# Compression products in column quarters and attention scores in row halves, in one hybrid decoder layer

## The chip, the cores and the metric

The kernel is one program on one core of a Trainium2 chip. The metric is device time in microseconds of one execution; lower is better. Five engines work side by side and in order, each on its own list of instructions: TensorE (PE in the profile, its weight loads PEld), VectorE (DVE), ScalarE (ACT), GpSimd (POOL) and SyncE (SP), which here issues nearly all loads from DRAM. TensorE is an array of 128 rows (the summed dimension) by 128 columns (the columns of the held operand, which become the partitions of the result). A product that holds only 32 columns can be put in one quarter of the array's columns, and one that sums over only 64 partitions in one half of its rows.

## The reference, cut to what matters

The layer takes 256 tokens of 1024 features: an adaptive norm, one input projection, a retention group of 4 heads, an attention group of 8 query heads in 2 groups of keys and values (NSA) with compressed, selected and windowed branches, one output projection, a second adaptive norm, and a retrieval over 16384 experts (PEER). The change touches two places of the attention group:

```
def _compress(kraw, pe, w1, b1, w2):
    ...
    blk = kraw[:, idx] + pe[None, None, :, None, :]
    blk = blk.transpose(0, 1, 3, 2, 4).reshape(B, ncb, G, CMP_LEN * DH)
    return jax.nn.gelu(blk @ w1 + b1) @ w2
...
s_s = jnp.einsum('bqghd,bgqnkd->bghqnk', qblk, ksel).astype(f32) * scale
...
s_w = jnp.einsum('bqghd,bkgd->bghqk', qblk, kwb).astype(f32) * scale
```

There are 15 overlapping blocks of 32 tokens in each of the 2 groups, so `blk @ w1` has 30 rows; it sums over 2048 features into 256, once for keys and once for values. A head has 64 features. With 256 tokens every block of the selected branch that a query may see is selected, so both branches become causal attention over all keys.

## The kernel before, in words

The program is in two parts. The prefix (about the first 184 us) makes the norm, the projections, retention, attention, the output projection and the second norm. PEER follows and streams 16 weights `wq`, then 128 `down` and 128 `up` weights through TensorE. All of it stands in one function, `build`; nearly every instruction is recorded by line 80, so the profile's groups are told apart by the names of tiles.

Most of the prefix's matrix products are made from two parts: a float32 weight `raw` is split on ScalarE into a rounded `H` and on VectorE into the rest `L`, and three products (`H` by `hH`, `L` by `hH`, `H` by `hL`) go to a bank of PSUM, tag `C`. These splits can be done ahead, and their products are what TensorE does while a chain elsewhere is under way. The compression, the attention and the transposes use plain float32 products; the trace has two records for each of those and one for each transpose.

`compress` (lines 537 to 595) runs for keys, then for values. Eight small products per half turn the projected rows into columns; VectorE adds the position table and makes `blk` (128 partitions by 16 by 30). Then 16 products, with 30 columns of `blk` held and 256 columns of a quarter of `w_cmp` (tile `praw`) streamed, sum into one bank of tag `O`. ScalarE copies the 30 x 256 result to `hn`, two transposes turn it, and a chain of small steps on VectorE and ScalarE (`cu`, `cw`, tanh, `hid`) makes the gelu. Two more sets of small products give the compressed keys `kcT`, or the compressed values `vc`, which are spread into `vblk`.

`attn_unit(tt, p)` (line 635) makes the scores of heads p and 4 + p for the 128 queries of half tt, for both branches. `keys` holds the keys of group 0 in partitions 0 to 63 and of group 1 in 64 to 127, each with zeros in the other 64 partitions. In the first half (tt = 0) one product of 512 columns gives all four blocks of scores in one bank of tag `S`; a second, small one with `identb` and `negm` adds the causal mask. In the second half there is one product of 512 columns for each group, in a bank of its own. VectorE takes the maxima (`a_mx`), ScalarE the exponentials (`a_pr`, one of each branch and group, with their sums), VectorE the scales `a_sm`, ScalarE applies them, TensorE transposes, ScalarE copies (`a_pT`), and `attn_pv` sums over the values into a bank of tag `O` with products that hold 64 columns: group 0 goes to partitions 0 to 63, group 1 to 64 to 127, in turn. There are two banks each of the tags `S`, `T`, `C` and `O`.

Each engine's order is fixed when the program is built: a scheduler takes what it holds to be ready by its own costs, except in stretches where the code asks for program order. Between the attention it places the products `C` of the retention's values and gate, the splits, and on VectorE the sums of the adaptive norm's weights (`adaraw`), 128 x 1024 each, whose results are needed only at the end of the prefix.

Of the kernel before, what the change touches and what calls it, by code (L numbers as in the profile page):

```python
# [36 lines left out]
P = 128  # L37
# [11 lines left out]
PRAW = 3  # L49
# [14 lines left out]
def build(tc, I, out, dbg=None, stop=None):  # L64
# [5 lines left out]
    class Ordered:  # L70
        """An engine whose instructions stay in program order while order["on"] has its name."""
# [74 lines left out]
    def mm(o, a, b, start, stop):  # L146
        PE.matmul(o, a, b, start=start, stop=stop)
# [6 lines left out]
    def rstd_of(pool, ss, n, inv, tag):  # L154
        """1/sqrt(ss * inv + eps), a square root and one Newton step."""
# [13 lines left out]
    def rstd_pair(pool, sa, sb, tag, between=lambda: None):  # L169
        """Two factors of 1/sqrt((sa + sb) / D + eps): a square root's inverse and one Newton step."""  # L170
# [15 lines left out]
    # ------------------------------------------------------------------ prefix  # L186
# [11 lines left out]
    def table(func, dep=None):  # L198
        """Has a function's table loaded before a chain needs it, once dep is there."""
        t = mk(pers, (P, 1), F32, "tinyo", bufs=2)  # L200
        S.activation(t, tiny if dep is None else dep, func, scale=0.0)
# [29 lines left out]
    # 2 silu(c) on every partition  # L231
# [36 lines left out]
    # norm 1: the product that transposes a row block scales it too  # L268
# [38 lines left out]
    # projection blocks A (q | kc ks kw vc) and B (rq | vs vw gate)  # L307
# [92 lines left out]
    def rope(dst, src, tab, tt, nh, dh, v=0):  # L400
        """dst (SBUF) = rotated src (PSUM), nh heads of dh."""
# [24 lines left out]
    def half(c, post, nf=0):  # L426
        """A projection block of 512 columns; post(i) after each of its four units."""
# [56 lines left out]

    rr = {}
# [23 lines left out]
    # NSA transposes  # L509
    qT = mk(pe_, (P, 4, T), F32, "qT")  # L510
    keys = mk(pe_, (P, 2, 2, T), F32, "keys")
    G.memset(keys[64:, 0], 0.0)
    G.memset(keys[:64, 1], 0.0)
    for tt in range(2):
# [3 lines left out]
        for g in range(2):  # L518
            rows = slice(g * 64, (g + 1) * 64)
            S.activation(keys[rows, g, :, tt * P:(tt + 1) * P], b[rows, :256].rearrange("p (a b) -> p a b", a=2),  # L520
                         AF.Copy)
# [10 lines left out]
    # compressed keys and values  # L532
# [4 lines left out]
    def compress(kv):  # L537
        pe_t, b1_t, w2_t = cmpc[kv]
# [7 lines left out]
        blk = mk(wk, (P, 16, 2, 15), F32, "blk", bufs=1)  # L546
        for s in range(2):
            rows = slice(s * 64, (s + 1) * 64)
            bv = b[rows, :].rearrange("p (g t) -> p g t", g=2)
            for g in range(2):  # L550
                src = bv[:, g, s:s + 1]
                src = bass.AP(tensor=src.tensor, offset=src.offset, ap=[list(src.ap[0]), [2, 16], [16, 15]])
                V.tensor_tensor(blk[rows, :, g, :], src, pe_t[rows, :, None].to_broadcast([64, 16, 15]), op=ALU.add)
        b = bank("O")
        for i in range(4):
            key = ("w" + kv, i)
            load(key, I["w" + kv + "1"][:, i * 4:i * 4 + 4, :], (P, 4, 256))
            r, _ = raws.pop(key)
            for q in range(4):
                mm(b[:30, :256], blk[:, i * 4 + q].rearrange("p a b -> p (a b)"), r[:, q * 256:(q + 1) * 256],  # L560
                   i == 0 and q == 0, i == 3 and q == 3)
        hn = mk(wk, (32, 256), F32, "hn", bufs=1)
        S.activation(hn[:30, :], b[:30, :256], AF.Copy)
        b = bank("O")
        for ch in range(2):
            PE.transpose(b[:, ch * 32:ch * 32 + 30], hn[:30, ch * P:(ch + 1) * P], ident[:30, :30])
# [30 lines left out]
    compress("k")  # L597
    compress("v")
# [8 lines left out]
    # NSA attention  # L607
# [27 lines left out]
    def attn_unit(tt, p):  # L635
        """The scaled probabilities of heads p and 4 + p, transposed."""
# [6 lines left out]
        bs = []  # L643
        if tt == 0:
            b = bank("S")
            mm(b.rearrange("p (a b) -> p a b", a=4), qT[:, p, tq], keys.rearrange("p a b c -> p (a b) c")[:, :, :P],
               True, False)
            mm(b, identb, negm.rearrange("p a b -> p (a b)"), False, True)
            V.tensor_reduce(mx, b.rearrange("p (a b) -> p a b", a=4), axis=AX.X, op=ALU.max, negate=True)
            bs = [b, b]  # L650
        else:
            for g in heads:
                b = bank("S")
                o = b.rearrange("p (a b) -> p a b", a=2)
                mm(b, qT[:, p, tq], keys[:, g].rearrange("p a b -> p (a b)"), True, False)
                mm(o[:, :, P:], identb, negm[:, :2, :], False, True)
                V.tensor_reduce(mx[:, g * 2:(g + 1) * 2], o, axis=AX.X, op=ALU.max, negate=True)
                bs.append(b)
        w = P * (tt + 1)
        for g in heads:  # L660
            pr = mk(wk, (P, 2, T), F32, "a_pr", bufs=7)
            for br in range(2):
                src = bs[g][:, g * 256 + br * P:g * 256 + br * P + P] if tt == 0 else bs[g][:, br * T:(br + 1) * T]
# [47 lines left out]
    # retention: scores transposed, decayed  # L711
# [14 lines left out]
    # retention: values, group norm, swish gate  # L726
# [43 lines left out]
    # output projection, residual, norm 2: one half of the tokens after the other  # L770
# [79 lines left out]
    # ------------------------------------------------------------------- PEER  # L850
# [61 lines left out]
    def top_gen(sc):  # L912
        """Top 16 of each product key half, then of each head's candidates; then the tables."""
# [7 lines left out]
        for tt in range(2):  # L921
# [30 lines left out]
            # softmax over the 16, its maximum first in the sorted values  # L952
# [368 lines left out]
```

## Time and profile before

| | us |
|---|---|
| median of 3 runs (1039.6 to 1041.15) | 1039.87 |
| span of the profiled execution | 1037.9 |
| TensorE busy | 1009.2 |
| VectorE busy | 760.4 |
| ScalarE busy | 606.8 |
| GpSimd busy | 61.5 |

The profiled execution's own time was not kept apart from the runs; its span lies 2.0 us under their median. A page reads from the top: which engine is busy for which share, then the span in slices, then the chain that ended last. An engine that is busy for 97% can still be paced by another in a stretch, so the stretches are read one by one.

### The profile page before, as it was taken

The numbers are of one execution on the slowest core, as the hardware profiler recorded it, in microseconds if no ns is written. First come the engines' busy times: TensorE is split into PE (matmuls) and PEld (weight loads), VectorE is DVE, ScalarE is ACT, GpSimd is POOL, SyncE is SP. The second block draws the span as 40 slices with busy tenths as digits, with TensorE's granted clock in tenths as the row PEclk, the third lists the DMA queues.
The fourth block names the chain that finished last, engine by engine and source line by source line (L and its number), as shares of the span: only waits on it lengthen the run. The fifth ranks groups of instructions, "written<-read, shape, count | busy, mean of one in ns | idle before, by whom it ended". The sixth has DMA issues, their size and how long they took to land.

```text
span 1037.9 us, 17713 instructions
## 1 busy us (share of the span) xinstructions
PE 1009.2 (97%) x6580; PEld 902.1 (87%) x6582; DVE 760.4 (73%) x1653; ACT 606.8 (58%) x1244; POOL 61.5 (6%) x53
## 2 busy tenths in 40 slices
PE   7999999999998889999999999999999999999995
PEld 6876687999998889999999999988888888888884
DVE  7988888899778786667777777665955556565665
ACT  7544884555436357777777777645445555545453
POOL 1040000000331310000000000000000000000001
PEclk9999999999999999999999999999999999999998
DMA  9998753546555444444444444567976666666661
GB/s 367 352 350 335 244 181 136 168 152 183 168 149 174 144 152 135 151 147 143 148 142 144 143 143 143 156 230 231 317 234 193 197 190 214 190 199 188 198 189 57
DMA packets 56184, 199.19 MB, mean 192 GB/s; under 512 B 7305, under 2 KB 7585, under 8 KB 55713
## 3 DMA queue, kind: packets, MB, share of 16 engines
q1 hardware_dynamic: 55200, 193.59, 58.3%
q0 software_dynamic: 752, 4.20, 1.1%
q8 instruction: 51, 0.84, 0.3%
q14 instruction: 37, 0.30, 0.1%
q10 hardware_dynamic: 144, 0.26, 0.1%
HBM read 195.92 MB, written 2.11 MB: 191 GB/s over the span
## 4 chain that ended last, share of the span: by engine, by line
PE 84%; DVE 9%; POOL 3%; ACT 1%; issue 1%; DMA 0%; SPq 0%; DVEq 0%; POOLq 0%; ACTq 0%
PE acc L80 54%; PE dn L80 9%; PE w L80 7%; PE C L80 5%; PE O L80 4%; POOL oe L946 3%; PE S L80 3%; PE T L80 2%; DVE ev L80 2%; DVE L L80 2%; DVE oh L80 1%; DVE tp L80 1%; DVE VL L80 1%; DVE adaraw L80 0%; DMA xn<-in_x_dram 0%
## 5 line engine op out<-in xcount | busy, mean ns | idle before, releaser
L80 DVE TENSOR_TENSOR L<-raw,H 128x1024 fp32r<-128x1024 f32 x284 | 346.4, 1221 | 119.5 <-ACT H L80 114.9
L80 ACT ACTIVATE H<-raw 128x1024 fp32r<-128x1024 f32 x284 | 300.0, 1058 | 172.4 <-PE acc L80 132.6
L80 PE MATMUL acc<-H,a 128*128 128x512 f32 (+1 forms) x1030 | 315.9, 388 | 0.0
L80 PE MATMUL acc<-hH,H 128*128 128x256 f32 x800 | 230.8, 289 | 0.0
L80 PE MATMUL acc<-hH,L 128*128 128x256 f32 x800 | 226.6, 283 | 3.3 <-DVE L L80 3.3
L80 PEld LDWEIGHTS acc<-H,a 128*128 128x128 f32 x1030 | 193.0, 188 | 39.9
L80 PE MATMUL acc<-hL,H 128*128 128x256 f32 x800 | 226.6, 283 | 0.0
L80 PE MATMUL acc<-L,a 128*128 128x512 f32 (+1 forms) x515 | 199.7, 388 | 0.0
L80 PEld LDWEIGHTS acc<-hH,L 128*128 128x128 f32 x800 | 152.9, 191 | 4.1 <-DVE L L80 4.1
L80 PEld LDWEIGHTS acc<-hH,H 128*128 128x128 f32 x800 | 153.5, 192 | 0.1
L80 PEld LDWEIGHTS acc<-hL,H 128*128 128x128 f32 x800 | 153.2, 192 | 0.2 <-DVE hL L80 0.2
L80 PEld LDWEIGHTS acc<-L,a 128*128 128x128 f32 x515 | 96.7, 188 | 19.7
L80 ACT ACTIVATE ow<-o,VL 128x128 f16<-128x128 f16 x256 | 104.5, 578 | 5.2 <-DVE o L80 5.2
L80 PE MATMUL dn<-hH,L 128*128 128x256 f32 x352 | 99.8, 283 | 4.4 <-DVE L L80 4.4
L80 PE MATMUL dn<-hH,H 128*128 128x256 f32 x352 | 101.5, 288 | 0.4 <-ACT H L80 0.4
L80 PE MATMUL dn<-hL,H 128*128 128x256 f32 x352 | 99.6, 283 | 0.0
L80 PEld LDWEIGHTS dn<-hH,L 128*128 128x128 f32 x352 | 67.3, 191 | 5.0 <-DVE L L80 5.0
L80 PE MATMUL w<-ow,o 128*128 128x128 f16 x512 | 71.0, 296 | 0.0
L80 PEld LDWEIGHTS dn<-hH,H 128*128 128x128 f32 x352 | 67.6, 192 | 0.6 <-ACT H L80 0.6
L80 PEld LDWEIGHTS dn<-hL,H 128*128 128x128 f32 x352 | 67.4, 192 | 0.0
L80 PEld LDWEIGHTS <-o 128*128 128x128 f16 x512 | 51.9, 118 | 3.4
L80 DVE TENSOR_TENSOR ow<-o,VL 128x512 f16<-128x512 f16 x64 | 26.9, 420 | 36.9 <-PE w L80 36.9
(333 smaller groups left out, 1213.5 us busy)
## 6 DMA issues: line engine op xcount, KB each, us to landing
raw<-in_down_dram SPq DMA_DIRECT2D x128, 512.0 KB, 3.6
raw<-in_up_dram SPq DMA_DIRECT2D x128, 512.0 KB, 3.7
adaraw<-in_wadaT_dram SPq DMA_DIRECT2D x40, 512.0 KB, 8.0
raw<-in_wq_dram SPq DMA_DIRECT2D x16, 512.0 KB, 3.7
raw<-in_win_C_dram SPq DMA_DIRECT2D x12, 512.0 KB, 5.2
rawA<-in_win_A_dram SPq DMA_DIRECT2D x8, 512.0 KB, 9.6
raw<-in_wout_dram SPq DMA_DIRECT2D x8, 512.0 KB, 4.7
VL<-in_wadaT_dram SPq DMA_DIRECT2D x8, 512.0 KB, 4.6
```

The lines of the kernel that those rows point to most:

```text
L80: i = fn(*a, **kw)
L946: G.tensor_tensor(oe, oh, cidx[:, p, :, None].to_broadcast([P, NCAND, 16]), op=ALU.mult)
```

## The change

In the compression the 30 columns become 32 (`blk` is padded with zeros), and there is a `blk` for keys and one for values. `blocks` makes both first. `compress_sums` then sums four things at once into the four quarters of one bank's partitions: keys, even and odd quarters of each weight block, and values, even and odd. There are still 32 products of 256 columns. The loads of `w_cmp_k1` and `w_cmp_v1` take turns, and their tiles have four buffers instead of three. ScalarE copies all 128 x 256 sums at once, and where the transposes stood a product with `sel4` (four unit matrices summed from `ident` on VectorE) adds the two partial sums and turns them.

In the attention `keys` loses its zeros. The scores of each group are one product over 64 partitions; group 0 lies in the upper half of the rows, group 1 in the lower, each with a bank of its own, in both halves of the queries. For tt = 0 they are 256 columns wide instead of one product of 512. The code issues both scores, then both masks.

```diff
-PRAW = 3
+PRAW = 4
...
+    sel4 = mk(pe_, (P, 32), F32, "sel4")
+    V.tensor_reduce(sel4, ident.rearrange("p (a b) -> p b a", a=4), axis=AX.X, op=ALU.add)
...
-    keys = mk(pe_, (P, 2, 2, T), F32, "keys")
-    G.memset(keys[64:, 0], 0.0)
-    G.memset(keys[:64, 1], 0.0)
+    keys = mk(pe_, (P, 2, T), F32, "keys")
...
-        for g in range(2):
-            rows = slice(g * 64, (g + 1) * 64)
-            S.activation(keys[rows, g, :, tt * P:(tt + 1) * P], b[rows, :256].rearrange("p (a b) -> p a b", a=2),
-                         AF.Copy)
+        S.activation(keys[:, :, tt * P:(tt + 1) * P], b[:, :256].rearrange("p (a b) -> p a b", a=2), AF.Copy)
...
-        blk = mk(wk, (P, 16, 2, 15), F32, "blk", bufs=1)
+        blk = mk(wk, (P, 16, 32), F32, "blk" + kv, bufs=1)
+        G.memset(blk, 0.0)
...
+    def compress_sums(blks):
+
         b = bank("O")
         for i in range(4):
-            key = ("w" + kv, i)
-            load(key, I["w" + kv + "1"][:, i * 4:i * 4 + 4, :], (P, 4, 256))
-            r, _ = raws.pop(key)
-            for q in range(4):
-                mm(b[:30, :256], blk[:, i * 4 + q].rearrange("p a b -> p (a b)"), r[:, q * 256:(q + 1) * 256],
-                   i == 0 and q == 0, i == 3 and q == 3)
-        hn = mk(wk, (32, 256), F32, "hn", bufs=1)
-        S.activation(hn[:30, :], b[:30, :256], AF.Copy)
+            rs = {}
+            for kv in "kv":
+                key = ("w" + kv, i)
+                load(key, I["w" + kv + "1"][:, i * 4:i * 4 + 4, :], (P, 4, 256))
+                rs[kv], _ = raws.pop(key)
+            for q2 in range(2):
+                for c, (kv, o) in enumerate((("k", 0), ("k", 1), ("v", 0), ("v", 1))):
+                    q = q2 * 2 + o
+                    PE.matmul(b[c * 32:(c + 1) * 32, :256], blks[kv][:, i * 4 + q], rs[kv][:, q * 256:(q + 1) * 256],
+                              start=i == 0 and q2 == 0, stop=i == 3 and q2 == 1, tile_position=(0, c * 32))
+        hn = mk(wk, (P, 256), F32, "hn", bufs=1)
+        S.activation(hn, b[:, :256], AF.Copy)
+        return hn
...
-            PE.transpose(b[:, ch * 32:ch * 32 + 30], hn[:30, ch * P:(ch + 1) * P], ident[:30, :30])
+            mm(b[:, ch * 32:ch * 32 + 30], hn[rows, ch * P:(ch + 1) * P], sel4[rows, :30], True, True)
...
-    compress("k")
-    compress("v")
+    blks = {kv: blocks(kv) for kv in "kv"}
+    hn2 = compress_sums(blks)
+    compress("k", hn2)
+    compress("v", hn2)
...
-        if tt == 0:
-            b = bank("S")
-            mm(b.rearrange("p (a b) -> p a b", a=4), qT[:, p, tq], keys.rearrange("p a b c -> p (a b) c")[:, :, :P],
-               True, False)
-            mm(b, identb, negm.rearrange("p a b -> p (a b)"), False, True)
-            V.tensor_reduce(mx, b.rearrange("p (a b) -> p a b", a=4), axis=AX.X, op=ALU.max, negate=True)
-            bs = [b, b]
-        else:
-            for g in heads:
-                b = bank("S")
-                o = b.rearrange("p (a b) -> p a b", a=2)
-                mm(b, qT[:, p, tq], keys[:, g].rearrange("p a b -> p (a b)"), True, False)
-                mm(o[:, :, P:], identb, negm[:, :2, :], False, True)
-                V.tensor_reduce(mx[:, g * 2:(g + 1) * 2], o, axis=AX.X, op=ALU.max, negate=True)
-                bs.append(b)
         w = P * (tt + 1)
+        bs = [bank("S") for g in heads]
+        for g in heads:
+            rows = slice(g * 64, (g + 1) * 64)
+            mm(bs[g][:, :2 * w], qT[rows, p, tq], keys[rows, :, :w], True, False)
+        for g in heads:
+            o = bs[g][:, :2 * w].rearrange("p (a b) -> p a b", a=2)
+            mm(o[:, :, w - P:], identb, negm[:, :2, :], False, True)
+            V.tensor_reduce(mx[:, g * 2:(g + 1) * 2], o, axis=AX.X, op=ALU.max, negate=True)
```

The scheduler lays out the prefix anew; from the second half of the output projection on, the order of every engine is the one of before. Three places follow.

TensorE, the end of the compression products (`blkk` and `blkv` are the padded columns of keys and values, `C` the retention's projection). Before, the last weight block of the keys:

```order
L80 MATMUL O_789<-praw_802,blk_784 30x256 x4
L80 MATMUL S_913<-qrT_582,krT_583 128x256
L80 MATMUL O_789<-praw_808,blk_784 30x256 x4
L80 MATMUL S_913<-qrT_582,krT_583 128x128
L80 MATMUL S_918<-qrT_582,krT_583 128x256
```

Now, the last weight block of both:

```order
L80 MATMUL C_1322<-H_1352,hH_144 128x512
L80 MATMUL O_803<-praw_840,blkk_782 32x256 x2
L80 MATMUL C_1321<-L_1353,hH_144 128x512
L80 MATMUL C_1321<-H_1352,hL_145 128x512
L80 MATMUL C_1322<-L_1353,hH_144 128x512
L80 MATMUL C_1322<-H_1352,hL_145 128x512
L80 MATMUL O_803<-praw_842,blkv_797 32x256 x2
L80 MATMUL O_803<-praw_840,blkk_782 32x256 x2
L80 MATMUL O_803<-praw_842,blkv_797 32x256 x2
```

The 32 products stood in runs of 1, 11, 4, 12 and 4; now they stand in runs of 2, 14, 2, 6, 2 and 6, and within a run the quarters alternate in pairs.

TensorE from the end of the compression to the first scores (`hid` is the hidden layer of keys, `S_957` and `S_958` the two halves' scores of the first unit, `S_995` those of the second). Now:

```order
L80 MATMUL C_1322<-H_1352,hL_145 128x512
L80 MATMUL O_868<-hid_859,w2k_616 64x15 x4
L80 MATMUL O_875<-sel_147_624,hn_852 128x30 x2
L80 MATMUL S_930<-kcT_770,qT_724 128x2x16 x4
L80 MATMUL S_957<-keys_725,qT_724 128x256
L80 LDWEIGHTS identb_570
L80 MATMUL S_957<-negm_572,identb_570 128x256
L80 MATMUL S_958<-keys_725,qT_724 128x256
L80 LDWEIGHTS identb_570
L80 MATMUL S_958<-negm_572,identb_570 128x256
L80 MATMUL S_995<-keys_725,qT_724 128x256
```

and VectorE at the same place, before and now (`sT` are the retention's scores, `cu`, `cw`, `hid` the keys' gelu):

```order
L80 TENSOR_SCALAR cu_819<-O_816,b1k_614 128x30 x2
L80 TENSOR_TENSOR sT_911<-S_918,xT_909 128x256
L80 TENSOR_TENSOR cw_820<-cu_819 128x60
L80 TENSOR_TENSOR sT_210_912<-S_918,xT_909 128x128
L80 TENSOR_SCALAR cw_820<-cw_820 128x60
L80 TENSOR_TENSOR cw_820<-cw_820,cu_819 128x60
L80 TENSOR_TENSOR sT_911<-S_923,xT_909 128x256
L80 TENSOR_SCALAR cw_820<-cw_820 128x60
L80 TENSOR_TENSOR sT_210_912<-S_923,xT_909 128x128
L80 TENSOR_TENSOR hid_821<-cw_820,cu_819 128x60
```

```order
L80 TENSOR_SCALAR cu_857<-O_854,b1k_614 128x30 x2
L80 SCALAR_TENSOR_TENSOR adaraw_1371,acc_117<-adaraw_1371,cs_98 128x1024
L80 TENSOR_TENSOR cw_858<-cu_857 128x60
L80 TENSOR_SCALAR cw_858<-cw_858 128x60
L80 TENSOR_TENSOR cw_858<-cw_858,cu_857 128x60
L80 SCALAR_TENSOR_TENSOR adaraw_1374,acc_117<-adaraw_1374,cs_98 128x1024
L80 TENSOR_SCALAR cw_858<-cw_858 128x60
L80 TENSOR_TENSOR hid_859<-cw_858,cu_857 128x60
```

Four small `sT` between the steps of the chain gave way to two sums `adaraw`; on TensorE the mask of each half stands right behind its score, so the two halves are not neighbours.

VectorE behind the attention (`mixNL` is the attention's result, `bst` and `mv` the statistics of the second half's retention, `woL` the rests of the output weights). Before and now:

```order
L80 TENSOR_TENSOR mixNL_906<-O_1120,mixNH_905 128x4x128
L80 TENSOR_TENSOR woL_397_1650<-raw_1647,woH_396_1649 128x1024
L80 BN_STATS bst_1466<-O_1457 128x6
L80 BN_STATS bst_1469<-O_1457 128x6
L80 BN_AGGR mv_1456<-bst_1466 128x2
```

```order
L80 TENSOR_TENSOR mixNL_903<-O_1133,mixNH_902 128x4x128
L80 SCALAR_TENSOR_TENSOR adaraw_1693,acc_117<-adaraw_1693,cs_98 128x1024
L80 TENSOR_TENSOR woL_400_1663<-raw_1660,woH_399_1662 128x1024
L80 BN_STATS bst_1479<-O_1470 128x6
L80 BN_STATS bst_1482<-O_1470 128x6
L80 BN_AGGR mv_1469<-bst_1479 128x2
```

One `adaraw` more stands between the attention's result and the statistics, and behind these (not shown) three `woL`, as before.

## Rows read from the trace of the kernel before

**Rows 1.** The page: busy time by engine, and the chain that ended last.

```profile
PE 1009.2 (97%) x6580; PEld 902.1 (87%) x6582; DVE 760.4 (73%) x1653; ACT 606.8 (58%) x1244; POOL 61.5 (6%) x53
...
PE 84%; DVE 9%; POOL 3%; ACT 1%; issue 1%; DMA 0%; SPq 0%; DVEq 0%; POOLq 0%; ACTq 0%
```

**Rows 2.** Stretches: from:to, length, busy us and instructions by engine, granted clock, DMA.

```profile
54.00:184.00 130.00, 127.46 (x764) 92.51 (x765) 110.10 (x259) 80.04 (x199) 13.11 (x12) 1.00 0.70 250
87.00:146.00 59.00, 58.77 (x356) 38.54 (x357) 50.25 (x124) 46.67 (x136) 0.00 (x0) 1.00 0.70 239
146.00:184.00 38.00, 35.89 (x222) 30.86 (x221) 30.91 (x70) 21.18 (x42) 2.12 (x3) 1.00 0.48 161
```

**Rows 3.** TensorE by time: start us, us from first start to last end, records.

```profile
70.37 0.62 PE L80 MATMUL O<-praw,blk 128*30 128x256 f32 x2
70.92 0.66 PE L80 MATMUL T<-ident,rn 128*128 128x128 f32 x4
71.50 4.93 PE L80 MATMUL O<-praw,blk 128*30 128x256 f32 x22
76.37 0.70 PE L80 MATMUL S<-qrT,krT 128*128 128x256 f32 x2
76.99 1.91 PE L80 MATMUL O<-praw,blk 128*30 128x256 f32 x8
```

**Rows 4.** Groups of TensorE in 54 to 185 us: records, busy us, mean ns.

```profile
L80 PE MATMUL O<-praw,blk 128*30 128x256 f32 x64 | 14.7, 381 | 0.0
```

**Rows 5.** TensorE by time: products holding 64 columns, and holding 128.

```profile
83.30 1.08 PE L80 MATMUL O<-ident,vcn 128*64 128x128 f32 x16
84.31 1.08 PE L80 MATMUL S<-kcT,qT 128*128 128x32 f32 x8
...
148.56 1.95 PE L80 MATMUL S<-ident,mod 128*128 128x128 f32 x16
150.34 1.06 PE L80 MATMUL O<-ident,mcol 128*128 128x128 f32 x8
```

**Rows 6.** TensorE by time: one score product of the second half and the next start.

```profile
105.93 1.02 PE L80 MATMUL S<-keys,qT 128*128 128x512 f32 x2
106.88 0.44 PE L80 MATMUL O<-cs_pT,vblk 128*64 128x128 f32 x4
```

**Rows 7.** SyncE by time, and the page's issues with the median us to landing.

```profile
66.84 0.33 SPq L80 DMA_DIRECT2D praw<-in_wk_dram  x1
...
praw<-in_wv_dram SPq DMA_DIRECT2D x4, 512.0 KB, 8.9
```

**Rows 8.** The keys' chain by time (ScalarE, TensorE), and the group of VectorE's sums.

```profile
78.94 0.37 ACT L80 ACTIVATE hn<-O 30x256 f32<-30x256 f32 x1 [5.26 <-PE O L80]
...
83.05 0.42 PE L80 MATMUL O<-hid,w2k 128*64 128x15 f32 x8
...
L80 DVE SCALAR_TENSOR_TENSOR adaraw<-adaraw,cs 128x1024 f32<-128x1024 f32 x24 | 28.7, 1216 | 0.0
```

**Rows 9.** VectorE and TensorE by time: a pair of `sT`, and neighbouring products `C`.

```profile
79.42 0.62 DVE L80 TENSOR_TENSOR sT<-S,xT 128x256 f32<-128x256 f32 x2 [1.37 <-issue]
...
61.42 0.39 PE L80 MATMUL C<-H,hH 128*128 128x512 f32 x1
61.65 0.39 PE L80 MATMUL C<-L,hH 128*128 128x512 f32 x1
```

**Rows 10.** The first unit's maxima (VectorE) and first exponential (ScalarE) by time.

```profile
87.04 0.69 DVE L80 TENSOR_REDUCE a_mx<-S 128x4 f32<-128x512 f32 x1 [0.79 <-remote]
...
87.77 0.37 ACT L80 ACTIVATE a_pr<-S,a_mx 128x128 f32<-128x128 f32 x1 [2.80 <-DVE a_mx L80]
```

**Rows 11.** Second half's retention by time: products, statistics, result, transposes.

```profile
146.09 1.95 PE L80 MATMUL O<-rv,sT 128*128 128x128 f32 x16
159.18 0.63 PE L80 MATMUL T<-ident,rn 128*128 128x128 f32 x4 [0.25 <-DVE rn L80]
...
148.07 0.50 DVE L80 BATCH_NORM_STATS2 bst<-O 128x6 f32<-128x128 f32 x2
...
158.35 0.69 DVE L80 SCALAR_TENSOR_TENSOR rn<-rn,sg 128x512 f32<-128x512 f32 x1
```

More of the change, by code (lines that the diff above doesn't have):

```diff
@@ L535, in build, with blocks @@
     vblk = mk(pe_, (P, 4, P), F32, "vblk")
-    def compress(kv):
-        pe_t, b1_t, w2_t = cmpc[kv]
+    def blocks(kv):
+        pe_t = cmpc[kv][0]
         b = bank("O")
@@ L545, in compress @@
                        True, True)
-        blk = mk(wk, (P, 16, 2, 15), F32, "blk", bufs=1)
+        blk = mk(wk, (P, 16, 32), F32, "blk" + kv, bufs=1)
+        G.memset(blk, 0.0)
+        bl = blk[:, :, :30].rearrange("p a (g c) -> p a g c", g=2)
         for s in range(2):
@@ L552, in compress @@
                 src = bass.AP(tensor=src.tensor, offset=src.offset, ap=[list(src.ap[0]), [2, 16], [16, 15]])
-                V.tensor_tensor(blk[rows, :, g, :], src, pe_t[rows, :, None].to_broadcast([64, 16, 15]), op=ALU.add)
+                V.tensor_tensor(bl[rows, :, g, :], src, pe_t[rows, :, None].to_broadcast([64, 16, 15]), op=ALU.add)
+        return blk
+    def compress_sums(blks):
         b = bank("O")
         for i in range(4):
-            key = ("w" + kv, i)
-            load(key, I["w" + kv + "1"][:, i * 4:i * 4 + 4, :], (P, 4, 256))
-            r, _ = raws.pop(key)
-            for q in range(4):
-                mm(b[:30, :256], blk[:, i * 4 + q].rearrange("p a b -> p (a b)"), r[:, q * 256:(q + 1) * 256],
-                   i == 0 and q == 0, i == 3 and q == 3)
-        hn = mk(wk, (32, 256), F32, "hn", bufs=1)
-        S.activation(hn[:30, :], b[:30, :256], AF.Copy)
+            rs = {}
[11 more added lines that the diff above has]
+        return hn
+    def compress(kv, hn):
+        pe_t, b1_t, w2_t = cmpc[kv]
         b = bank("O")
+        rows = slice(0, 64) if kv == "k" else slice(64, P)
         for ch in range(2):
-            PE.transpose(b[:, ch * 32:ch * 32 + 30], hn[:30, ch * P:(ch + 1) * P], ident[:30, :30])
+            mm(b[:, ch * 32:ch * 32 + 30], hn[rows, ch * P:(ch + 1) * P], sel4[rows, :30], True, True)
         u = mk(wk, (P, 2, 30), F32, "cu")
@@ L642, in attn_unit @@
         prs = []
-        bs = []
-        if tt == 0:
-            b = bank("S")
-            mm(b.rearrange("p (a b) -> p a b", a=4), qT[:, p, tq], keys.rearrange("p a b c -> p (a b) c")[:, :, :P],
-               True, False)
-            mm(b, identb, negm.rearrange("p a b -> p (a b)"), False, True)
-            V.tensor_reduce(mx, b.rearrange("p (a b) -> p a b", a=4), axis=AX.X, op=ALU.max, negate=True)
-            bs = [b, b]
-        else:
-            for g in heads:
-                b = bank("S")
-                o = b.rearrange("p (a b) -> p a b", a=2)
-                mm(b, qT[:, p, tq], keys[:, g].rearrange("p a b -> p (a b)"), True, False)
-                mm(o[:, :, P:], identb, negm[:, :2, :], False, True)
-                V.tensor_reduce(mx[:, g * 2:(g + 1) * 2], o, axis=AX.X, op=ALU.max, negate=True)
-                bs.append(b)
-        w = P * (tt + 1)
+        w = P * (tt + 1)
+        bs = [bank("S") for g in heads]
[6 more added lines that the diff above has]
+            V.tensor_reduce(mx[:, g * 2:(g + 1) * 2], o, axis=AX.X, op=ALU.max, negate=True)
         for g in heads:
@@ L662, in attn_unit @@
             for br in range(2):
-                src = bs[g][:, g * 256 + br * P:g * 256 + br * P + P] if tt == 0 else bs[g][:, br * T:(br + 1) * T]
+                src = bs[g][:, br * w:(br + 1) * w]
                 S.activation(pr[:, br, :w], src, AF.Exp, bias=mx[:, g * 2 + br:g * 2 + br + 1],
```

## The prediction

> **What bounds the kernel now.** I read the page first: TensorE is busy for 1009 of 1037.9 us and makes 84% of the chain that ended last [rows 1]. Then the table by stretches, for the part that the change touches. From 54 to 184 us TensorE is busy 127.46 of 130, at a granted clock of 1.00, the upper of its two levels, 2.4 GHz [rows 2]. So it paces the prefix, and a microsecond of product that goes is at first a microsecond won: the rest of the program keeps its order on every engine, so that whatever time the prefix ends earlier or later moves the end alike. But the second number in that row to see is VectorE's 110.10 of 130, and between 87 and 146 us, the attention, 50.25 of 59 beside ScalarE's 46.67 [rows 2]. These two have only some 9 and 12 us to spare there. If TensorE's list gets shorter by much, the chains through them are what comes next. The span is 2.0 us under the median of the runs; I work in differences and put them on the median.
>
> **Compression products.** Before, 64 records take 14.7 us busy [rows 4]; in a run 22 records need 76.37 - 71.50 = 4.87 us, 0.22 each, or 0.44 a product [rows 3], so 32 products take 14.1 us. Now quarters may run beside each other. The trace shows this for halves: 16 records that hold 64 columns, alternating between the halves, take 84.31 - 83.30 = 1.01 us, while 16 that hold 128 columns and stream the same 128 take 150.34 - 148.56 = 1.78 us [rows 5], a factor of 1.76 of the possible 2. In the new order the runs are of 2, 14, 2, 6, 2 and 6 products, in which the fullest quarter holds 1, 4, 1, 2, 1 and 2: 11 product times, 4.84 us, and with the halves' 88% 5.5 us. A run also costs at its ends: the two lone records of 70.37 take 0.55 us to the next start where 0.44 would do, and the four transposes behind them 0.58 where they need 0.44 (4 x 0.11, half of what 8 of rows 5 would take): 0.25 a run [rows 3]. There are six runs where there were five. The gain is 14.1 - 5.5 - 0.25 = **8.3 us**; it is nothing, less 0.25, if quarters take turns, and 9.0 if they overlap fully. I take 8.3, by the nearest row.
>
> **Scores.** Before, 12 products of 512 columns at 106.88 - 105.93 = 0.95 us, 11.4 us in all [rows 6]. Now there are 8 of 256 and 8 of 512 columns; each alone lasts as its columns ask, 8 x 0.475 + 8 x 0.95 = 11.4 us again. Only two neighbours in different halves could share the time, and in the new order a mask, which uses all rows, stands between the halves in seven of eight pairs. The last pair may save 0.9 us. So that part of the change mostly doesn't do what it says. Against it, fifteen lone runs in a new shape of the array: no row of before shows a product over 64 rows beside full ones. From below, such an end costs nothing and the sum is -0.9; from above it costs what a column run does, 15 x 0.25 = +3.8 and no pair overlaps. I take the middle, **+1.5 us**. The Trainium skill speaks against the change here ("TensorEngine Tiling (Array Packing)", Key Properties): a change of tiling mode drains TensorE, where staying in a mode does not. It gives no price. The 0.25 us of rows 3 agrees for columns; for rows nothing here shows it. By that rule the upper end would hold, and the sum below would be 2.3 us more.
>
> **What costs nothing.** The products with `sel4` are four of 30 columns where four transposes were, two tenths at most. GpSimd clears `blk` where it cleared `keys`, at the start, when it idles; ScalarE has three copies less. The reduction for `sel4` and four maxima more on VectorE are under 1 us together. The loads are in time: in SyncE's list the last weight block of the values now stands three places behind where, before, a load was issued at 66.84, and a load of this kind lands after 8.9 us [rows 7], so by about 80 us, before TensorE gets there. No load waits for a product any more.
>
> **The keys' chain.** Before, the keys' sums ended first, and the values' 14 products' work lay ready to cover the gelu of the keys. Now both end together, at about 86 us (71.5, plus 5.5 and 1.5 for the runs, 2.9 for retention scores, 21 products `C` at 0.23 [rows 9]), and nothing of the values covers. From the copy `hn` to the first product with `hid` it took 83.05 - 78.94 = 4.1 us [rows 8]. Two `adaraw` of 1.2 us [rows 8] now stand in that chain on VectorE, and four `sT`, about 1.1 us by the pair of rows 9, left it: 5.4 us. TensorE has six `C` and two small products meanwhile, 1.4 + 0.3. The wait is **3.7 us** (0 if VectorE's steps come free earlier, 5 at most), and behind it in TensorE's list stand the compressed scores and all attention.
>
> **Banks of scores.** A unit of the first half took one of two banks `S`; it now takes both. So the next unit's first score waits until ScalarE has finished with the first bank: a maximum of a half (some 0.35 us of the 0.69), the delay to ScalarE (87.77 - 87.04 - 0.69 is under 0.1), and two exponentials of 0.35 [rows 10], with other steps between them on ScalarE. TensorE has only the other half, 0.6 us, to do. In the new order nothing else stands between the first two units, and again little before the first unit of the second half. I take two waits of 1.25 us, **2.5 us** (0 to 5).
>
> **Behind the attention.** From the retention's products at 146.09 to the transposes of their result at 159.18 there were 13.1 us, filled: TensorE waited 0.25 [rows 11]. Of VectorE's part, 148.07 to 159.04, 11.0 us, the gate's products (1.8 us) are now done earlier, which leaves 9.2; but `mixNL`, one `adaraw` and one `woL`, 3.0 us, stand ahead, and ScalarE's copy 0.7 ahead of them: 12.9 us. TensorE's list between the two places is now 16 records (1.8), 21 products `C` and four transposes (4.8 + 0.4), and 26 records of broadcasts (2.9), 9.9 us. The wait is **3.0 us** (0 to 4).
>
> The sum: -8.3 + 1.5 + 0.2 + 3.7 + 2.5 + 3.0 = +2.6 us, less the 0.25 that TensorE waited there before [rows 11], **+2.4**: 1039.87 + 2.4 = 1042.3 us.
>
> **Rivals.** *The products decide.* If TensorE stays as full as before, 127.46 of 130, because VectorE and ScalarE run ahead where they have room, only about half of one of the three waits remains: -8.3 + 1.7 + 2.7 = -3.9, 1036 us. For it: before, the same scheduler left 2.5 us of idle TensorE in the whole stretch. Against: TensorE's list gets 6.6 us shorter, VectorE's doesn't, and VectorE had 9 us to spare in the attention. It decides from where the three waits sum to under 4.6 us. *The waits come about in half:* 4.6 + 1.5 puts it within 2 us of before, 1040. *Quarters take turns:* then TensorE reaches the keys' chain some 8 us later, part of it in place of waits: 1047 us. Against it stand the halves of rows 5. *Every change of shape drains:* the upper end of the scores, +2.3, and longer chains: 1045 us. For it the 0.25 us of rows 3. *Halves of rows overlap across the masks:* seven pairs would save 7 x 0.7 = 5 us, 1037 us; against it, a mask sums over all 128 rows of the array.
>
> **How the numbers follow.** Forecast 1042.3, chance 0.38; drains 1045, 0.10; quarters in turn 1047, 0.05; half the waits 1040, 0.25; products decide 1036, 0.18; halves overlap 1037, 0.04. A measurement of this kernel can tell 0.2%, 2.1 us, from no change. So slower 0.53, same 0.25, faster 0.22. The range goes from 1035.8, which takes in the two faster cases, to 1047.5; some 2 in 10 lie outside, the gain of the products without any wait (1033) below and quarters in turn with all waits above.
>
> **What would show it.** In the changed trace: the 64 records of the compression in some 6 to 7.5 us by their runs, with overlapping starts within a run; the score products alone, 0.95 us or more for 512 columns, their starts not in pairs but for the last; TensorE waiting some 3 to 4 us for `hid` near 87 to 91 us, on `a_pr` at the second unit's scores, and on `rn` ahead of the output projection; PEER's first product later by 2.4 us. It is wrong if TensorE waits less than 4.6 us in all, or if a product over 64 rows is cheaper than its columns say.

## The result, and the profile after

The changed kernel takes 1052.02 us (median of four, 1051.2 to 1052.89) against 1039.74 before (1039.6 to 1041.15): a ratio of 1.0112, 95% interval 1.0098 to 1.0127. It is slower by 12.3 us, where 2.4 were forecast and 7.6 allowed for.

The page of the changed kernel, busy time and chain, answers to [rows 1]:

```profile
PE 1016.8 (97%) x6598; PEld 905.9 (86%) x6598; DVE 761.6 (72%) x1658; ACT 603.9 (57%) x1241; POOL 60.5 (6%) x53
...
PE 84%; DVE 9%; POOL 3%; ACT 2%; issue 1%; DMA 0%; SPq 0%; DVEq 0%; POOLq 0%; ACTq 0%
```

TensorE is busier by 7.6 us, although the compression products take less of it. The table by stretches says where (from:to, length, busy us and instructions by engine, granted clock, DMA); its rows answer to [rows 2]:

```profile
54.00:184.00 130.00, 123.45 (x717) 85.78 (x716) 102.56 (x243) 74.42 (x184) 11.01 (x9) 0.93 0.67 240
87.00:146.00 59.00, 55.29 (x282) 33.77 (x283) 45.28 (x117) 39.78 (x122) 0.31 (x1) 0.86 0.62 217
146.00:184.00 38.00, 35.17 (x218) 28.96 (x218) 31.67 (x72) 24.69 (x45) 0.00 (x0) 1.00 0.46 151
```

The last column but two is the one to see: the granted clock, 1.00 in all three rows of before, is 0.86 in the attention. TensorE by time, and the same stretch in steps of 4 us:

```profile
87.43 0.40 PE L80 MATMUL C<-H,hL 128*128 128x512 f32 x1
90.75 0.42 PE L80 MATMUL O<-hid,w2k 128*64 128x15 f32 x8 [2.92 <-issue]
91.09 0.65 PE L80 MATMUL O<-sel,hn 64*128 64x30 f32 x4
91.67 1.91 PE L80 MATMUL S<-kcT,qT 128*128 128x32 f32 x8
93.52 1.22 PE L80 MATMUL S<-keys,qT 64*128 64x256 f32 x2
...
108.90 0.48 PE L80 MATMUL C<-H,hL 128*128 128x512 f32 x1
```

```profile
88.00:92.00 4.00, 1.25 (x14) 1.19 (x14) 2.76 (x11) 0.61 (x3) 0.00 (x0) 0.95 0.61 187
92.00:96.00 4.00, 4.00 (x13) 2.55 (x12) 1.66 (x9) 0.44 (x3) 0.00 (x0) 0.50 0.55 216
96.00:100.00 4.00, 4.00 (x14) 1.90 (x14) 3.42 (x11) 3.20 (x13) 0.00 (x0) 0.50 0.00 0
100.00:104.00 4.00, 4.00 (x13) 2.35 (x10) 3.12 (x10) 3.11 (x11) 0.31 (x1) 0.50 0.64 197
104.00:108.00 4.00, 4.00 (x10) 2.15 (x9) 0.59 (x3) 0.81 (x4) 0.00 (x0) 0.50 1.01 411
108.00:110.00 2.00, 1.98 (x7) 1.02 (x8) 0.82 (x4) 0.30 (x2) 0.00 (x0) 0.84 0.24 96
```

TensorE stands idle for 2.92 us until `hid` is there (the profile names no releaser; VectorE's `hid` ends at 90.64 us), does its small products of 15, 30 and 32 columns, and from about 91.6 to 108.6 us it runs at 0.50, the lower of its levels, 1.2 GHz. It counts as busy all that time, with 10 to 14 records in 4 us where the stretch before the change has 23 (128 in 22 us). The eight products with `kcT` take 1.85 us to the next start, and took 0.92 before (from 84.31 [rows 5] to 85.23 us). This is what no term of the prediction held. A second such stretch of 3.4 us stands at 194 us, behind the wait for `dg`. The waits of TensorE in 54 to 200 us (what waited and for whom, us in total, times, longest):

```profile
PE O L80 <- issue: 2.9, 1, 2.9
PE T L80 <- DVE dg L80: 2.0, 1, 2.0
PE C L80 <- DVE woL L80: 1.9, 2, 1.1
PE O L80 <- ACT a_pT L80: 1.2, 2, 0.9
PE S L80 <- ACT a_pr L80: 0.3, 1, 0.3
```

The span of the profiled execution, the slowest of the four, grew by 13.2 us, from 1037.9 to 1051.1. PEER's first product comes 12.3 us late, so the prefix holds all of that but 0.9 us. Before, and then changed:

```profile
183.15 0.74 PE L80 MATMUL acc<-hH,H 128*128 128x256 f32 x4
...
195.45 1.20 PE L80 MATMUL acc<-hH,H 128*128 128x256 f32 x4
```

To divide these 12.3 us I took all records of TensorE from 65.8 us to that product and counted each from its start to the start of the next, less idle time before the next, and half of it where the clock was 0.50; the other half is the loss to the clock. In us:

| | before | changed | quarters alone | halves alone | changed, wait filled |
|---|---|---|---|---|---|
| compression products | 14.4 | 5.5 | 5.5 | 14.4 | 5.5 |
| scores with masks | 12.2 | 13.9 | 12.5 | 13.7 | 14.1 |
| other products | 88.1 | 92.2 | 91.7 | 90.4 | 93.9 |
| products nobody reads | | | | | 2.8 |
| idle | 2.5 | 8.5 | 9.6 | 3.0 | 4.9 |
| lost to the half clock | 0 | 9.3 | 5.1 | 0 | 1.7 |
| PEER's first product at | 183.15 | 195.45 | 190.29 | 187.40 | 188.85 |

The last three columns are runs below (e2, e3, e6). In the changed kernel the products gave back 3.2 us; idle time took 6.0, and the clock 9.3. The view by stretches bears that out: before and after, from 65.8 us to that product, busy 114.81 of 117.35 and 121.14 of 129.65, at 1.00 and 0.93.

```profile
65.80:183.15 117.35, 114.81 (x709) 82.63 (x707) 98.95 (x238) 75.17 (x192) 6.54 (x8) 1.00 0.69 243
```

```profile
65.80:195.45 129.65, 121.14 (x729) 84.54 (x727) 100.85 (x244) 73.64 (x188) 7.33 (x8) 0.93 0.62 219
```

### The profile page after: what moved, and what is told of

Read it like the earlier page. It is cut to its first block, busy times and chain, and to the rows that moved or that the text cites. A ratio compares the mean times of both kernels' runs of the same rounds, so it can differ in the third digit from the quotient of the medians.

```text
span 1051.1 us, 17740 instructions
## 1 busy us (share of the span) xinstructions
PE 1016.8 (97%) x6598; PEld 905.9 (86%) x6598; DVE 761.6 (72%) x1658; ACT 603.9 (57%) x1241; POOL 60.5 (6%) x53
## 4 chain that ended last, share of the span: by engine, by line
PE 84%; DVE 9%; POOL 3%; ACT 2%; issue 1%; DMA 0%; SPq 0%; DVEq 0%; POOLq 0%; ACTq 0%
PE acc L80 54%; PE dn L80 9%; PE w L80 7%; PE C L80 6%; PE O L80 3%; PE S L80 3%; POOL oe L953 3%; PE T L80 2%; DVE L L80 2%; DVE ev L80 2%; DVE oh L80 1%; DVE tp L80 1%; DVE adaraw L80 1%; DVE VL L80 1%; DMA xn<-in_x_dram 0%
```

## The experiments

Three theories were tried at first: the wait for `hid` costs the clock; the thin products behind it (half the rows, or 15 to 32 columns) cost it; or the clock is a bystander and the chains on VectorE and ScalarE set the pace. All ratios are to the kernel before, in runs on the same chip.

**Filling the wait.** e1 puts 12 products that nobody reads ahead of the first product of `hid`, e6 six (`range(6)` in the same line):

```diff
         b = bank("O")
         if kv == "k":
+            for _ in range(12):
+                mm(b[:, 256:512], hn[:, :P], hn, True, True)
+        if kv == "k":
             for g in range(2):
```

> The changed kernel with 12 products more, that nobody reads (hn by hn, 256 columns, about 0.22 us each, 2.7 us in all), queued on TensorE ahead of the first product of hid, where it stood idle from 87.8 to 90.75 us. Theory 'the wait costs the clock': with the idle time filled the granted clock stays at 1.00 through 87 to 120 us, the 17.4 us at half the clock give back about 8.7 us, and the time falls from 1052 to 1042 to 1045 us. Rival 'the shapes cost the clock' (the products over 64 rows and over 15, 30 and 32 columns behind the wait): the clock falls at about 92 us all the same, and the time stays at 1050 or above. Rival 'the clock is a bystander' (the chains on VectorE and ScalarE set the pace from 91 to 110 us): the clock stays at 1.00 but the time stays at 1049 to 1052 us.

> The changed kernel with 6 unread products ahead of the first of hid, which took 0.45 us each in the run with 12 of them, so 2.7 us, about the idle time that they replace. Theory 'the wait costs the clock': 1.00 from 87 to 120 us, and 1043 to 1046 us: the 12 of the run before took 5.4 us in place of 2.9, and that excess of 2.5 us is gone. Rival 'the clock is a bystander': 1048 us or above, as with 12.

e1: 1048.19 us (1.0076, 1.0059 to 1.0093). e6: 1046.74 us (1.0066, 1.0050 to 1.0083). In both the clock stays at 1.00 from 88 to 110 us; e6 by time, and by stretches:

```profile
86.41 2.86 PE L80 MATMUL O<-hn 128*128 128x256 f32 x12
90.18 0.42 PE L80 MATMUL O<-hid,w2k 128*64 128x15 f32 x8
91.10 1.05 PE L80 MATMUL S<-kcT,qT 128*128 128x32 f32 x8
```

```profile
65.80:188.85 123.05, 118.11 (x738) 83.14 (x737) 99.62 (x243) 73.54 (x188) 6.85 (x8) 0.98 0.64 229
88.00:110.00 22.00, 20.39 (x116) 12.39 (x116) 18.48 (x55) 13.46 (x50) 0.00 (x0) 1.00 0.72 241
```

The same half-row products now run at the full clock. So work that computes nothing made the kernel 5.3 us faster, which rules out the shapes alone and the bystander. It is less than expected: e1's fillers took 5.4 us, two records each, not 2.7, and in e6 the other products grew by 1.7 us; the scheduler placed them in another order, which may be why.

**One part alone.** e2 has the new compression with the old keys and scores, e3 the reverse.

> The compression products in quarters alone; keys and scores as before. Theory 'the wait costs the clock': the wait for hid is there as in the changed kernel (2.5 to 3.2 us), the clock falls to 0.50 behind it, and the time is 1047 to 1051 us, slower than the kernel before although 8.6 us of products are gone. Rival 'the shapes cost the clock': without half-row products the clock stays at 1.00 and the time is 1035 to 1039 us (before 1039.7, less 8.6, with 2.9 for the wait and 0 to 3 behind the attention). Rival 'the clock is a bystander': 1047 to 1051 us too, but with the clock at 1.00.

> The scores in two halves of the rows alone, with keys that are not padded; compression as before. Theory 'the wait costs the clock': no wait of over 1 us on TensorE from 54 to 146 us, the clock stays at 1.00 there, and the time is 1039 to 1043 us (before 1039.7, with 0.9 to 1.5 for the products and up to 2.5 for the waits on the S banks). Rival 'the shapes cost the clock': the clock falls to 0.50 at the first half-row products and the time is 1046 to 1050 us.

e2: 1047.48 us (1.0067, 1.0050 to 1.0083). e3: 1044.65 us (1.0041, 1.0026 to 1.0055). e3 by stretches, and e2 by time:

```profile
65.80:187.40 121.60, 118.59 (x726) 83.43 (x724) 101.36 (x244) 73.77 (x189) 7.52 (x9) 1.00 0.68 237
```

```profile
90.61 0.42 PE L80 MATMUL O<-hid,w2k 128*64 128x15 f32 x8 [2.92 <-issue]
```

In e3 the half-row products leave the clock at 1.00 and cost TensorE time: 1.5 us for scores and masks, 2.3 us for other products; e3 is slower than the upper end that I had expected. e2 came out as the first theory had it: the same wait as in the changed kernel is followed by the half clock, but for 6.8 us, not 17. Each part alone loses.

**Shortening the wait.** In e5 and e7 two of VectorE's sums `adaraw` stand behind `hid`, not in its chain; e5 is the changed kernel, e7 the quarters alone.

```diff
-    def filler(n=1):
-        for _ in range(n):
+    def filler(n=1, after=None):
+        for k in range(n):
             if rest:
-                with (tc.issue_after(last["L"].ins) if FAFTER else ExitStack()):
+                with (tc.issue_after(last[after].ins) if after and k else ExitStack()):
                     ada(rest.pop(0))
...
-        V.tensor_tensor(hid, w, u, op=ALU.mult)
+        last["hid" + kv] = V.tensor_tensor(hid, w, u, op=ALU.mult)
...
-            filler(nf)
+            filler(nf, {1: "hidk", 2: "hidv"}.get(i) if nf == NF1 else None)
```

> The changed kernel with two of the weighted sums on VectorE (adaraw, 1.22 us each) that stood between cu and hid of the keys put behind hid, and one pair behind hid of the values; nothing is added, and TensorE's order around the wait is that of the changed kernel. The wait for hid shrinks from 2.9 to 0.4 to 0.8 us. Theory 'the wait costs the clock': the clock stays at 1.00 from 87 to 120 us, and besides the 2.4 us the 8.5 us that the 17 us at half the clock cost come back, less 1 to 2 us that turn into other waits: 1041 to 1044 us. Rival 'the shapes cost the clock': it falls at about 92 us as in the changed kernel, and only the wait itself comes back: 1048 to 1050 us. Rival 'the clock is a bystander': 1.00, but 1048 to 1050 us.

> The compression in quarters alone, with the two sums put behind hid. Theory 'the wait costs the clock': the wait of 2.9 us and the 9 us at half the clock behind it go, 1047.5 becomes 1041 to 1043 us; more than that is not to be had, since the waits behind the attention (4 to 6 us) have VectorE's and ScalarE's work behind them. Rival 'the shapes cost the clock': 1044.5 to 1045.5 us, the wait alone.

e5: 1049.52 us (1.0097, 1.0080 to 1.0114). e7: 1045.97 us (1.0061, 1.0041 to 1.0081). First e5, by time and then by stretches:

```profile
89.01 0.42 PE L80 MATMUL O<-hid,w2k 128*64 128x15 f32 x8 [1.16 <-issue]
```

```profile
88.00:110.00 22.00, 20.60 (x91) 12.04 (x92) 17.15 (x50) 12.15 (x48) 0.31 (x1) 0.77 0.64 218
```

And e7, in the same two views:

```profile
89.11 0.42 PE L80 MATMUL O<-hid,w2k 128*64 128x15 f32 x8 [1.16 <-issue]
```

```profile
88.00:110.00 22.00, 19.14 (x108) 12.22 (x110) 19.64 (x57) 15.06 (x59) 0.00 (x0) 1.00 0.69 242
```

This felled the simple form of my theory: with 1.16 us in place of 2.92 the clock in e5 still fell, at 90.0 us for 10 us, and both runs are slower than the theory gave. In e7, with the same wait but scores over all rows, the profiled run keeps the full clock behind `hid`. The four runs of e7 go from 1044.42 us at a mean clock of 0.992 to 1048.45 at 0.988, so it is at the lower level for longer in some executions than in others; where in the program, runs without a trace don't tell. Thin products without a wait did not lower the clock (e3, e6). Behind the same wait, half-row scores went with a longer stretch at half the clock (17 us against 6.8 in e2, 10 in e5 against none in e7). Which of the thin products counts for how much was not separated, and e10 below shows that they are not needed.

**Filling with work of the kernel's own.** e4 is e1's fill on the quarters alone. e9 and e10 are e7 with the first two score units, or the first one, written ahead of the keys' chain (the diff is e9's; e10 has `range(1)`):

```diff
...
+    ahead += [attn_unit(0, p) for p in range(2)]
+    compress("k", hn2)
+    compress("v", hn2)
     nsa(0)
```

> The compression products in quarters alone, with the same 12 products in the wait for hid. Theory 'the wait costs the clock': clock 1.00 through 87 to 120 us and 1036 to 1041 us (before 1039.7, less 8.6, with 3.5 for fillers and what they displace, and 0 to 3 behind the attention), the fastest of the four and 7 us or more below the same kernel without fillers. Rival 'the shapes cost the clock': as without fillers, 1035 to 1039 us. Rival 'the clock is a bystander': 1047 to 1051 us, as without fillers.

> The compression in quarters alone (scores as before), the sums on VectorE behind hid, and the first two score units written ahead of the chain of the compressed keys, so that their products, maxima and exponentials lie in the time in which TensorE waited for hid and kcT. Theory 'TensorE has to stay busy there': no wait of over 0.5 us and no half clock from 80 to 130 us in the profile, runs closer together than the 4 us of the kernel without this (1044.4 to 1048.5), and 1040 to 1043 us. Rival 'VectorE and ScalarE bound the attention' (each busy for 24 of the 26 us from 120 to 146): the waits come back behind the attention, and the time is 1043 to 1046 us even with the full clock.

> The same with the first score unit alone ahead of the chain, so that one bank of S stays free for the retention products. 'TensorE has to stay busy': 1040 to 1044 us, between the kernel without this (1046.0) and the one with two. 'VectorE and ScalarE bound the attention': 1043 to 1046 us.

e4: 1044.92 us (1.0036, 1.0021 to 1.0050), above what I expected. e9: 1049.47 (1.0085, 1.0068 to 1.0102), with a wait of 2.0 us for `hid` again and 10 us of half clock from 91 us, although its scores are over all rows; why two units are worse than none I did not follow up. e10: 1042.75 (1.0024, 1.0015 to 1.0034), with the full clock from 88 to 110 us. There the next wait shows, on VectorE's gate products, with 6.8 us at half the clock from 147 us (the profiled run, 1043.7 us, is one of the slower of ten). By time, and by stretches:

```profile
148.45 0.80 PE L80 MATMUL C<-woH,mixNH 128*128 128x512 f32 x1 [3.71 <-DVE sg L80]
```

```profile
150.00:152.00 2.00, 2.00 (x7) 1.51 (x6) 2.00 (x3) 0.05 (x1) 0.00 (x0) 0.50 0.00 0
```

The products behind this wait hold 128 columns, sum over all 128 rows and stream 512 columns, and they run at 0.50 all the same.

**Halves next to one another.** In e8 (changed kernel, sums behind `hid`), e11 (that with two units ahead) and e12 (halves alone), a product of one column takes each of a unit's banks, and the two halves follow.

```diff
-            mm(bs[g][:, :2 * w], qT[rows, p, tq], keys[rows, :, :w], True, False)
+            got = PE.matmul(bs[g][:, :1], qT[rows, p, tq], keys[rows, 0, :1], start=True, stop=True)
+        with tc.issue_after(got.ins):
+            for g in heads:
+                rows = slice(g * 64, (g + 1) * 64)
+                mm(bs[g][:, :2 * w], qT[rows, p, tq], keys[rows, :, :w], True, False)
```

> As the changed kernel with the sums behind hid, and the two half-row products of each score unit side by side on TensorE: a product of one column takes each of the unit's two banks first, and the halves follow one another at once (16 such small products more). If halves that follow one another overlap, as the one adjacent pair of the changed kernel showed (1.07 us for both, where one alone took 1.05), the score products fall from 12 to 6 or 7 us with 1 to 1.5 us for the small ones, and the time is 3 to 4 us below the same kernel without pairs: 1038 to 1041 us. If holding both banks until the pair can start makes TensorE wait for the exponentials instead, the time is that of the kernel without pairs or up to 3 us above it.

> All of the change with the halves of a score unit next to one another, the sums behind hid, and two score units ahead of the chain. The run with pairs alone had 8 us of its 10 us loss as half clock near 90 and 146 us. 'TensorE has to stay busy': most of that comes back, 1039 to 1043 us. 'VectorE and ScalarE bound the attention': 1043 to 1046 us, with the waits behind the attention at 5 us or more.

> The scores in halves alone, with the halves next to one another, and the compression as before. In the run without pairs the 32 half-row products took 12.4 us of TensorE where the 24 full ones took 11.2; side by side, with the small products that take the banks, 9.7 us as in the other run with pairs. If that is all, 1044.65 becomes 1041 to 1042.5 us, and the clock stays at 1.00. If holding two banks makes TensorE wait for the exponentials, 1044 to 1047 us.

e8: 1046.67 us (1.0060, 1.0043 to 1.0077). e11: 1044.48 (1.0040, 1.0026 to 1.0054). e12: 1047.03 (1.0063, 1.0046 to 1.0080). e8 by time, a whole unit of the second half with its two small products:

```profile
141.04 1.35 PE L80 MATMUL S<-keys,qT 64*128 64x1 f32 x8
142.33 0.39 PE L80 MATMUL S<-negm,identb 128*128 128x256 bf16 x2
```

So halves that meet do overlap, 1.29 us for what takes 2.1 apart, and scores with masks fell from 13.9 us in e5 to 11.4 in e8. The two profiled runs hide what that is worth: idle time and half clock are 13.4 us in e5's and 15.0 in e8's, but e5's is the fastest of its four and e8's the slowest. In the medians e8 is 2.85 us below e5, near the 3 to 4 us expected, and no run of e8 (1046.27 to 1048.32 us) is as long as the shortest of e5 (1048.5 to 1052.1). The time itself missed its range because e5, from which it was reckoned, is longer than was thought.

In e11 and e12 not all pairs met: scores with masks took 13.6 and 13.9 us, no less than e3's 13.7, and idle time in e12 rose by 1.4 us over e3. e11's time lies in the range given for VectorE and ScalarE as the bound, but the waits of 5 us behind the attention that were to show it are not there (the longest is 1.0 us). Its waits for `hid` and `kcT` are short, and from 94 us it has 6.8 us of half clock none the less:

```profile
92.11 0.42 PE L80 MATMUL O<-hid,w2k 128*64 128x15 f32 x8 [0.78 <-ACT cw L80]
...
94.44 1.92 PE L80 MATMUL S<-kcT,qT 128*128 128x32 f32 x8 [0.77 <-ACT kcT L80]
```

**The waits behind the attention.** e13 is e10 with three `adaraw` and two `woL` put behind `sg`; e14 adds 8 unread products in the wait for `dg`, where nothing else moves (the last four lines of the diff; the first two are a part of e13).

```diff
+        with (tc.issue_after(last["sg"].ins) if k >= 6 else ExitStack()):
             V.tensor_tensor(l, r, f(h), op=ALU.subtract)
...
+            spare = bank("S")
+            with tc.issue_after(sh.ins):
+                for _ in range(8):
+                    mm(spare[:, :P], ident, ident, True, True)
```

> As the run with one unit ahead, with three of VectorE's weighted sums and two low parts of the output weights put behind the two products sg, which free the banks that the output projection waits for. In that run TensorE waited 3.7 us for sg at 144.7 us, and 6.8 us at half the clock followed, 3.4 us lost. 'Idle TensorE costs twice, as the wait and as the clock': the wait falls to 1.5 to 2.5 us, less half clock behind it, 1042.75 becomes 1038 to 1041 us. If the sums only move the wait to the products of mod (their sums end later): 1042 to 1044 us.

> The same, with 8 unread products of 128 columns (1.8 us) in TensorE's wait of 1.95 us for dg ahead of the second half of norm 2, where the order is fixed and nothing else moves; there 3.4 us at half the clock followed in that run, 1.7 us lost. If the idle time is what costs the clock: no half clock at 184 to 192 us, 1 to 2 us below the run without. If the clock is a matter of what follows, or the time is lost anyway: no difference within 0.5 us.

e13: 1041.61 us (1.0011, 1.0002 to 1.0020). e14: 1041.22 (1.0007, 0.9998 to 1.0016). e13 is just above its range: the wait for `sg` fell to 2.9 us only. For `dg`, e13 by time, and by stretches:

```profile
183.33 2.61 PE L80 MATMUL T<-dg,xm 128*128 128x128 f32 x16 [1.95 <-DVE dg L80]
```

```profile
184.00:188.00 4.00, 4.00 (x24) 4.00 (x23) 2.09 (x4) 2.15 (x3) 0.00 (x0) 0.58 0.91 315
```

And e14:

```profile
182.24 2.05 PE L80 MATMUL T<-dg,xm 128*128 128x128 f32 x16 [0.17 <-DVE dg L80]
```

```profile
184.00:188.00 4.00, 4.00 (x33) 3.81 (x32) 2.28 (x5) 1.66 (x4) 0.00 (x0) 1.00 0.61 238
```

In the profiled runs the fill keeps the clock. In the medians it is worth 0.4 us, which is within the intervals of both and, by what was expected, no difference. e13's eleven runs go from 1040.73 us, at a mean clock of 0.996, to 1043.45, at 0.988, and that one is the run profiled, so its trace overstates what the wait for `dg` costs in the median; e14's runs go from 1041.04 to 1041.80. No version beat the kernel before; the best is level with it.

**What the traces show together.** Where TensorE waited 0.78 us or more for `hid`, the clock fell behind it in six of seven traces (the changed kernel, e2, e5, e8, e9, e11; not e7); where that wait is not there, in none of nine (the kernel before, e1, e3, e4, e6, e10, e12, e13, e14). So at this place the fall came only with idle time, and the fills show that it is the cause. It is not all that decides. The wait for `dg` is in every version but e14, 1.8 to 2.3 us long with the same products on either side, and in or behind it the clock fell in nine traces (the changed kernel, e1, e4, e5, e6, e9, e10, e11, e13) and stayed at 1.00 in six (the kernel before, e2, e3, e7, e8, e12). From the kernel before:

```profile
PE T L80 <- DVE dg L80: 1.9, 1, 1.9
```

In e4 that wait is 1.96 us, TensorE's order around it is record for record that of before, and 3.4 us at half the clock follow. What else decides stays open.

## Why the prediction was wrong

The direction was right, and so were the two largest terms, the compression products and the keys' chain. Going through its steps:

- **Compression products, -8.3.** Right: 14.4 us became 5.5 by the count above, -8.9. Starts of two quarters lie 0.01 us apart, and four records go every 0.21 us, where before one took 0.22 [rows 3]. TensorE by time:

```profile
74.43 0.39 PE L80 MATMUL O<-praw,blkv 128*32 128x256 f32 x2
74.44 0.39 PE L80 MATMUL O<-praw,blkk 128*32 128x256 f32 x2
74.64 0.39 PE L80 MATMUL O<-praw,blkv 128*32 128x256 f32 x2
```

- **Scores, +1.5.** Near, and in part by luck: the scores alone cost 1.0 us more, and the masks, now one for each half in both halves of the queries, 0.8, which the term left out. A lone half of 512 columns takes 1.06 us to the next start, not 0.95 [rows 6], one of 256 columns 0.63, not 0.475, and the pair at the end 1.07 for both:

```profile
110.23 0.70 PE L80 MATMUL S<-keys,qT 64*128 64x256 f32 x2
110.86 0.44 PE L80 MATMUL T<-ident,a_pr 128*128 128x128 f32 x2
...
125.20 1.12 PE L80 MATMUL S<-keys,qT 64*128 64x512 f32 x2
126.26 0.28 PE L80 MATMUL S<-negm,identb 128*128 128x256 bf16 x1
...
141.71 1.13 PE L80 MATMUL S<-keys,qT 64*128 64x512 f32 x4
142.78 0.39 PE L80 MATMUL S<-negm,identb 128*128 128x256 bf16 x2
```

 The Trainium skill says ("TensorEngine Tiling (Array Packing)", Key Properties) that a change of tiling mode drains TensorE. The trace agrees with it: a lone half takes 0.11 us (512 columns) to 0.16 us (256) more than its columns by [rows 6]. The 0.25 of [rows 3] was too much.
- **What costs nothing, +0.2.** Too small. The products with `sel4` cost 0.6 us more than the transposes did, and all products besides compression and scores 4.0 us more. By the same count the transposes of `a_pr` and the products with `a_pT` and `cs_pT` have 2.1 us of that, and the products `C` 0.3. The new order takes those with `a_pT` and `cs_pT` in 39 runs where there were 28; that shorter runs are the reason is argued, not tested.
- **The keys' chain, 3.7.** Right in place and nearly in size: 2.92 us.
- **Banks of scores, 2.5.** Not there: `S` waited 0.3 us in the changed kernel, and e3, with its full clock, lists no wait of `S` at all.
- **Behind the attention, 3.0.** Right in size, 2.8 us (0.9 for `a_pT`, 1.9 for `woL`), wrong in whom it waits for: not on `rn`. So the size is luck.
- **The step that failed** is the sum itself. It took every duration from rows at a clock of 1.00 [rows 2] and counted each wait at its own length, though it forecast 9.2 us of new idle time and named the products queued behind the first of it. 6.0 us of idle came, and the clock took 9.3 us more. Put into the prediction's own sum, that gives -8.9 + 1.7 + 4.0 + 6.0 + 9.3 = +12.1; the other 0.2 of the 12.3 us lie in the record under way at 65.8 us. Of the rivals none had this; "the products decide" was refuted by 8.5 us of idle time, "quarters take turns", at 1047 the nearest, by the 5.5 us of the compression, and "drains", at 1045, by 0.11 to 0.16 us a lone half.
- **Sums of two rivals.** "The waits come about in half" adds up to -8.3 + 1.7 + 4.6 = -2.0, so 1037.9 us and not 1040; and half of one wait is at most 1.85, not the 2.7 of "the products decide". The miss does not hang on either.

The last 0.9 us lie behind the prefix, where the forecast had any shift go through alike. All changed versions show 3.4 to 6.8 us at half the clock that begin between 319 and 331 us, the profiled run of before none; over all versions the prefix-to-end time differs from before by -0.4 to +1.5 us, so this stays open.

## What to carry to other kernels

When products get cheaper, list what TensorE waits for next, and price each new wait together with what runs behind it: here the clock behind a wait of 2.92 us, with thin products behind it, cost 8.5 us (half of 17) besides. Work that was spread out covers chains; making two groups of products end at the same moment uncovers the chain behind them, so try what else can stand in the gap, and measure it: one score unit ahead was worth 3.2 us (e10 against e7), two cost 3.5 (e9). And halves of the array pay only where the scheduler lets them meet: an instruction over all rows between them takes the gain away.

## What the runs showed of the hardware

In the prefix TensorE's granted clock fell to its lower level in or behind waits of 1.2 to 3.7 us, once (e11) behind two of 0.8, and stayed there for 3.4 to 17 us while the engine counted as busy; before the change, waits of up to 1.9 us in the prefix left it at 1.00. Nor is it fixed for one program: e7's four executions had mean clocks of 0.992, 0.991, 0.989 and 0.988 and took 1044.42, 1044.88, 1047.05 and 1048.45 us. And filling a wait of 2.9 us with products that nobody reads made a kernel 5.3 us faster.
